# Time mixing: small triangles inverted as two halves at once, and the block between them by two products

## The chip, the cores and the metric

The kernel runs on one core of a Trainium2 chip. What counts is the device time of one execution in microseconds, as the median of several runs. The engines of a core are named as in the profile: PE is TensorE (PEld its weight loads), DVE is VectorE, ACT is ScalarE, POOL is GpSimd, SP is SyncE, which issues the transfers.

## The reference

Two layers of a streaming encoder, for a prompt of 1024 frames with 16 meta tokens ahead of it and for 64 frames of a running stream. Each layer projects the normalised input, sends the columns through three groups of heads side by side (a gated convolution, latent attention, time mixing), and projects the results back:

```python
z = h @ w_in
xin, bg, cg, ga, cq, ckv, kr, gb, zc, gc = jnp.split(z, IN_OFFSETS, axis=-1)
y_a = bg * conv * jax.nn.silu(ga)
y_b = o.reshape(b, t, MLA_W) * jax.nn.silu(gb)
y_c = yn.reshape(b, t, RWKV_W).astype(x.dtype) * jax.nn.silu(gc)
y = jnp.concatenate([y_a, y_b, y_c], axis=-1) @ w_out
return x + y
```

The change is in time mixing, a recurrence over the tokens with 4 heads of 64 by 64 state:

```python
def step(s, inp):
    r_t, w_t, k_t, v_t, kk_t, a_t = inp
    sa = jnp.einsum('bhvk,bhk->bhv', s, -kk_t)
    s = (s * w_t[:, :, None, :] + sa[..., None] * (kk_t * a_t)[:, :, None, :]
         + v_t[..., None] * k_t[:, :, None, :])
    return s, jnp.einsum('bhvk,bhk->bhv', s, r_t)
```

## The kernel before, in words

All tokens of both streams lie side by side, 1104 columns in three groups of up to 384 (`GROUPS`, line 36), features on the partitions. A layer begins with the projection (`project`, line 469): one block of 128 output columns for one token group is 24 matmuls into the tile `prj`, over 8 slices of the input with float32 split into a high and a low part (`whi`, `wlo`, `hhi`, `hlo`). The weights of a block come as `wraw`, and ScalarE and VectorE make `whi` and `wlo` of it. In `inproj_rest` (line 519) the blocks follow one another: the rest of the time mixing columns, gates, the latent columns `cq` and `ckv`, the rotary key `kr` (with `krt` and the weight `wkr`), the convolution (`xin`, `u`, `cv`), gates.

Time mixing runs beside this stream of projections. It is done in chunks of 64 tokens, in closed form within a chunk, and the chunks are chained by the state. `rwkv` (line 886) has three streams for it: `rwkv_prep` (line 922) prepares six parts a layer (three token groups of six chunks, for two pairs of heads), `rwkv_scan` walks the state through them (`xp`, `sp`, `state`, at the end `yp`), `rwkv_finish` does the group norm (`wq<-yp`, `gs`, then the turn `ym`). There are so 12 preparations in the kernel; they are counted here from the first of layer 0 to the twelfth, the seventh to twelfth being those of layer 1.

A preparation has to invert, for each of 12 chunk and head pairs, a unit upper triangular matrix of 64 by 64. It is done in levels. The four diagonal blocks of 16 by 16 come first: VectorE adds them out of the masked product into `dg` (line 1040), a trip through DRAM (`scr`) turns them round into `tri`, in which each of 48 partitions holds one 16 by 16 triangle, VectorE inverts them by rows (lines 1066 to 1070, 28 instructions for the 14 steps n), POOL sets the diagonal to one (line 1071), a copy makes the transpose, and another trip through DRAM brings both back as `dq` (named `dg` in the rows, whose tile it takes) and `dt`. VectorE spreads them with a mask to the block diagonal matrices `Q` (`wq<-dg`) and `Tm` (`wa<-dt`). Then TensorE joins blocks of 16 to 32 and 64 by products (`inv`), of which the first, `prod(A, Tm)` (line 1099, `inv<-wa` in the rows), needs `Tm`:

```python
        o = prod(A, Tm, self.psp("inv"))
```

What sets the order of the work: the kernel is written out by a Python program that keeps a model of each engine's time (`Meter`, lines 91 to 200). Each stream yields what its next step needs; `pump` (line 260) is called after each matmul of the projections and lets a stream of time mixing go on once the model says that what it needs is there. So the model decides how many `prj` matmuls stand between `tm<-cst,wb` (the last turn before the inversion, line 1063) and `inv<-wa`. On VectorE, ScalarE, POOL and SP the instructions are put in order once more when the program is built, by that framework's own estimate, so that the 28 do not stand in one piece.

The tile `lora` (line 929, one buffer) holds the two low-rank inputs of decay and learning rate. SP loads it at the start of a preparation, ScalarE passes half of it through a sigmoid in three steps, VectorE scales it, and two products read it; after them the preparation of before doesn't need it any more. `tri` and `lora` have one buffer each; attention, which comes later, uses both in turn for its weights.

Of the kernel before, what the change touches and what calls it, by code (L numbers as in the profile page):

```python
# [15 lines left out]
ALU = mybir.AluOpType  # L16
AX = mybir.AxisListType
# [14 lines left out]
GN = 384  # L32
# [4 lines left out]
BLK = 16  # L37
# [157 lines left out]
class Net:  # L195
# [726 lines left out]
    def rwkv_prep(self, l, i, g, hp):  # L922


        nc, I, O = self.nc, self.I, self.O
        tag = self.rwkv_tag(i)
        S = lambda s: self.S(tag, s)
        gc = slice(GN * g, GN * (g + 1))
        lora = self.small("lora", [128, 512])[:, :GN]
        nc.sync.dma_start(lora, self.zd[6, :, gc])  # L930
        wl = lora[0:64]
        self.sigmoid(wl, wl, 2.0)
# [2 lines left out]
        r, k, v = (wr[:, GN * x:GN * (x + 1)] for x in range(3))  # L935
# [14 lines left out]
        def turned(src, ts=range(3)):  # L950

            ps = rp("tm")
            for x, t in enumerate(ts):
                self.tr(ps[:, 128 * x:128 * (x + 1)], src(t), self.c(C_ID, 128))
            return ps[:, :GN].rearrange("p (t f) -> p t f", f=128)
# [3 lines left out]
        for t in range(3):  # L959
# [3 lines left out]
                                in0=ps[:, :GN].rearrange("p (t f) -> p t f", f=128),  # L963
                                in1=self.w0b[:, hc].unsqueeze(1).to_broadcast([128, 3, 128]), op=ALU.add)
# [16 lines left out]
        for t in range(3):  # L981
            tri = self.c(C_TRI0 if g == 0 and t == 0 else C_TRI, 128)
# [54 lines left out]
        for j in range(2):  # L1037
# [4 lines left out]
                                op=ALU.add, axis=AX.X)  # L1042
        scr = nc.dram_tensor(f"tri{l}_{g}_{hp}", (3, 6, 8, BLK, BLK), F32).ap()
        nc.sync.dma_start(scr[0].rearrange("t b r k -> (b r) t k"), dg)
        tri = self.small("tri", [128, 512])[:48].rearrange("p (i r k) -> p i r k", i=2, k=BLK)
        nc.sync.dma_start(tri[:, 0], scr[0].rearrange("t b r k -> (t b) r k"))
        yield kt, "rw"
        for ts in ((0, 1, 2), (3, 4, 5)):
            o = turned(lambda t: wx[:, 128 * t:128 * (t + 1)], ts)
# [10 lines left out]
        o = turned(lambda t: v[:, 128 * t:128 * (t + 1)])  # L1060
# [2 lines left out]
        nc.scalar.activation(at, turned(lambda t: wb[:, GN * t:GN * t + 128]), AF.Copy)  # L1063

        up, tm = tri[:, 0], tri[:, 1]
        for n in range(1, BLK - 1):
            o = [48, n, BLK - 1 - n]
            nc.vector.tensor_tensor(out=tm[:, :n, n + 1:], in0=up[:, :n, n:n + 1].to_broadcast(o), in1=up[:, n:n + 1, n + 1:].to_broadcast(o),
                            op=ALU.mult)
            nc.vector.tensor_tensor(out=up[:, :n, n + 1:], in0=up[:, :n, n + 1:], in1=tm[:, :n, n + 1:], op=ALU.add)  # L1070
        nc.gpsimd.memset(tri[:, 0].rearrange("p r k -> p (r k)")[:, 0:BLK * BLK:BLK + 1], 1.0)
        nc.vector.tensor_copy(tm, up.rearrange("p r k -> p k r"))
        nc.sync.dma_start(scr[1:3].rearrange("x t b r k -> (t b) x r k"), tri)
        dq, dt = dg, self.small("dt", [128, 6, BLK])
# [10 lines left out]
        def prod(lhs, rhs, ps, cc=slice(0, 64)):  # L1085
            o = ps[:, :GN].rearrange("p (t n) -> p t n", n=64)
            for t in range(6):
                for c in range(2):
                    self.mm(o[cr(c), t, cc], lhs[cr(c), t, :], rhs[cr(c), t, cc], start=True, stop=True)
            return o  # L1090
# [8 lines left out]
        o = prod(A, Tm, self.psp("inv"))  # L1099
# [13 lines left out]
        o = [x[:, :GN].rearrange("p (j t n) -> p j t n", j=2, n=64) for x in ps]  # L1113
# [13 lines left out]
        o = lambda c, j, x: ps[c][cr(j), 192 * x:192 * (x + 1)].rearrange("p (t n) -> p t n", n=64)  # L1127
        for j in range(2):
            for t, c in quad:
                b = cr(1 - c)  # L1130
# [404 lines left out]
```

## Time and profile before

| | us |
|---|---|
| median of 3 runs (1551.71 to 1553.72) | 1553.61 |
| the profiled execution, its own time | 1553.56 |
| its span in the profile | 1551.8 |
| PE busy (95% of the span, 12060 instructions) | 1476.9 |
| DVE busy (69%, 2623 instructions) | 1065.6 |
| ACT busy (50%) | 769.8 |
| POOL busy (17%) | 256.5 |

The profile is of one execution. The span runs from the first to the last instruction that it shows. Busy time is the time in which an engine had an instruction under way; PE's instructions overlap, so that a matmul of 384 columns lasts 0.34 us in a row and the next begins 0.175 us after it. The time in brackets behind a row is how long the engine was idle just before, and what ended that. Names are those of the program's tiles without numbers (`wq<-dg,cst` writes `wq` and reads `dg` and `cst`); nearly all instructions carry line 81, that of a helper, so tiles and shapes tell them apart. [...]

### The profile page before, as it was taken

To read this page: it belongs to the slowest core of one execution; us is meant where nothing else is said; L and a number is where in the kernel's file an instruction comes from. 1 tells how busy PE (TensorE), PEld (TensorE's weight loads), DVE (VectorE), ACT (ScalarE), POOL (GpSimd) and SP (SyncE) were. 2 spreads that over 40 slices of the span, in tenths; PEclk is the share of its full clock that TensorE was granted. 3 is DMA by queue.
4 is the path that set the end of the run, shared out by engine and by line. 5 is a ranking of instruction groups with operands and counts; after the bars stand their busy time and mean duration, and the time that the engine had idled before them with its cause. 6 is when DMAs were issued, how large, how long until landed. Compare 5 with 4: busy or idle time off the path is not lost.

```text
span 1551.8 us, 30755 instructions
## 1 busy us (share of the span) xinstructions
PE 1476.9 (95%) x12060; PEld 1311.2 (84%) x12060; DVE 1065.6 (69%) x2623; ACT 769.8 (50%) x1842; POOL 256.5 (17%) x281
## 2 busy tenths in 40 slices
PE   7999998998999999999999998899999999999996
PEld 7988887987887878879999887798988878778795
DVE  7576596675868766675845575776867787676566
ACT  7135454444577565563522354444356775565442
POOL 0221221311221101100011222312212301011002
PEclk9999999999999999999999999999999999999998
DMA  6332112222324101211323311212222331102123
GB/s 218 123 113 68 52 54 60 83 52 57 92 94 152 38 26 33 68 57 62 147 93 103 110 45 49 70 48 81 69 65 65 115 120 46 31 19 84 47 65 117
DMA packets 95328, 119.82 MB, mean 77 GB/s; under 512 B 41872, under 2 KB 74768, under 8 KB 95184
## 3 DMA queue, kind: packets, MB, share of 16 engines
q1 hardware_dynamic: 95184, 117.87, 24.6%
q8 instruction: 95, 1.56, 0.4%
q14 instruction: 49, 0.40, 0.1%
HBM read 81.24 MB, written 36.60 MB: 76 GB/s over the span
## 4 chain that ended last, share of the span: by engine, by line
PE 65%; DVE 17%; ACT 7%; issue 5%; DMA 3%; POOL 2%; SPq 0%; DVEq 0%; POOLq 0%; ACTq 0%
PE prj L81 31%; PE sc L81 7%; PE po L81 7%; PE tr L81 5%; PE upq L81 3%; DVE tri L81 3%; PE inv L81 2%; DVE wq L81 2%; PE val L81 1%; DVE wlo L81 1%; ACT wq L81 1%; PE upk L81 1%; DVE st L81 1%; DVE cv L81 1%; PE w L81 1%
## 5 line engine op out<-in xcount | busy, mean ns | idle before, releaser
L81 PE MATMUL prj<-hhi,whi 128*128 128x384 f32 (+1 forms) x1152 | 391.7, 340 | 7.5 <-ACT hhi L81 6.6
L81 PE MATMUL prj<-hlo,whi 128*128 128x384 f32 (+1 forms) x1152 | 390.7, 339 | 0.6 <-DVE hlo L81 0.6
L81 PE MATMUL prj<-hhi,wlo 128*128 128x384 f32 (+1 forms) x1152 | 390.4, 339 | 0.2 <-DVE wlo L81 0.2
L81 PEld LDWEIGHTS prj<-hhi,whi 128*128 128x128 f32 x1152 | 218.9, 190 | 11.0 <-ACT hhi L81 6.6
L81 PEld LDWEIGHTS prj<-hlo,whi 128*128 128x128 f32 x1152 | 218.7, 190 | 4.9 <-DVE hlo L81 1.0
L81 PEld LDWEIGHTS prj<-hhi,wlo 128*128 128x128 f32 x1152 | 218.7, 190 | 3.3 <-issue 0.5
L81 PE MATMUL prj<-yhi,wo 128*128 128x384 f32 (+2 forms) x776 | 207.0, 337 | 0.9 <-DVE xn L81 0.9
L81 PE MATMUL sc<-ka,qa 128*128 128x264 f32 (+8 forms) x720 | 152.4, 334 | 2.3 <-ACT p L81 2.0
L81 ACT ACTIVATE p<-sc,st 128x144 f32<-128x144 f32 (+8 forms) x240 | 128.1, 542 | 50.4 <-DVE st L81 49.3
L81 PEld LDWEIGHTS prj<-yhi,wo 128*128 128x128 f32 x776 | 138.4, 188 | 4.8 <-DVE xn L81 2.4
L81 DVE TENSOR_REDUCE st<-sc 128x1 f32<-128x144 f32 (+8 forms) x240 | 118.0, 502 | 24.3 <-PE sc L81 22.4
L81 PE MATMUL prj<-ylo,wo 128*128 128x384 f32 (+2 forms) x388 | 130.6, 337 | 0.0
L81 ACT ACTIVATE pt<-tr 128x512 f32<-128x512 f32 (+3 forms) x172 | 90.0, 544 | 77.6 <-PE tr L81 76.3
L81 PEld LDWEIGHTS sc<-ka,qa 128*128 128x128 f32 (+1 forms) x720 | 112.2, 187 | 19.0 <-ACT p L81 6.1
L81 PE MATMUL tr<-cst,p 128*128 128x128 f32 (+2 forms) x752 | 115.7, 277 | 3.3 <-ACT pt L81 1.7
L81 PE MATMUL po<-pt,v 128*64 128x256 f32 (+3 forms) x864 | 110.7, 357 | 0.0
L81 PEld LDWEIGHTS tr<-cst,p 128*128 128x128 f32 (+2 forms) x752 | 83.5, 140 | 25.6 <-issue 7.6
L81 POOL TENSOR_TENSOR qa<-qt,qa 128x512 fp32r<-128x512 f32 (+1 forms) x40 | 47.3, 1184 | 349.3 <-ACT qa L81 349.3
L81 ACT ACTIVATE whi<-wraw 128x1024 fp32r<-128x1024 f32 x48 | 50.7, 1056 | 82.6 <-PE prj L81 64.9
L81 DVE TENSOR_TENSOR tri<-tri 48x14 f32<-48x14 f32 (+6 forms) x336 | 82.2, 245 | 9.1 <-DMA tri<-tri 0.3
L81 PEld LDWEIGHTS po<-pt,v 128*64 128x64 f32 (+1 forms) x864 | 56.6, 136 | 33.5 <-issue 11.6
L81 DVE TENSOR_SCALAR p<-p,st 80x336 f32<-80x336 f32 (+5 forms) x144 | 81.5, 568 | 1.9
(227 smaller groups left out, 2639.9 us busy)
## 6 DMA issues: line engine op xcount, KB each, us to landing
wraw<-w_in SPq DMA_DIRECT2D x48, 512.0 KB, 3.6
wraw<-w_out SPq DMA_DIRECT2D x32, 256.0 KB, 2.6
zd<-z SPq DMA_DIRECT2D x14, 576.0 KB, 3.4
wr<-zd SPq DMA_DIRECT2D x36, 192.0 KB, 3.0
gd<-gate SPq DMA_DIRECT2D x12, 552.0 KB, 3.1
yraw<-yd SPq DMA_DIRECT2D x8, 552.0 KB, 4.0
xn<-x SPq DMA_DIRECT2D x8, 552.0 KB, 3.9
xd<-xn SPq DMA_DIRECT2D x8, 552.0 KB, 3.0
```

What stands on the lines that cost most here:

```text
L81: r = f(*args, **kw)
```

## The change

The triangle of 16 by 16 is taken as two of 8 by 8 on the diagonal and a block of 8 by 8 between them. The row by row steps run over both halves in the same instruction (6 steps n, 12 instructions). The block between is then multiplied by the one inverse and by the other: each product is one multiplication of 512 elements a partition and one reduction over the last 8, 4 instructions. The scratch for all of this is the tile `lora`, of which the first 48 partitions are used; before, the scratch was the half `tm` of `tri` itself. The memset of the diagonal stands ahead of the loop, since the products need it.

```diff
-        lora = self.small("lora", [128, 512])[:, :GN]
+        room = self.small("lora", [128, 512])
+        lora = room[:, :GN]
...
         up, tm = tri[:, 0], tri[:, 1]
-        for n in range(1, BLK - 1):
-            o = [48, n, BLK - 1 - n]
-            nc.vector.tensor_tensor(out=tm[:, :n, n + 1:], in0=up[:, :n, n:n + 1].to_broadcast(o), in1=up[:, n:n + 1, n + 1:].to_broadcast(o),
-                            op=ALU.mult)
-            nc.vector.tensor_tensor(out=up[:, :n, n + 1:], in0=up[:, :n, n + 1:], in1=tm[:, :n, n + 1:], op=ALU.add)
-        nc.gpsimd.memset(tri[:, 0].rearrange("p r k -> p (r k)")[:, 0:BLK * BLK:BLK + 1], 1.0)
+        flat, room = tri.rearrange("p i r k -> p (i r k)"), room[:48]
+        nc.gpsimd.memset(flat[:, 0:BLK * BLK:BLK + 1], 1.0)
+        h = BLK // 2
+        two = flat[:, 0:2 * (h * BLK + h)].rearrange("p (b x) -> p b x", b=2)[:, :, 0:h * BLK].rearrange("p b (r k) -> p b r k", k=BLK)[:, :, :, 0:h]
+        for n in range(1, h - 1):
+            o = [48, 2, n, h - 1 - n]
+            part = room[:, 0:2 * n * (h - 1 - n)].rearrange("p (b r k) -> p b r k", b=2, r=n)
+            nc.vector.tensor_tensor(out=part, in0=two[:, :, :n, n:n + 1].to_broadcast(o), in1=two[:, :, n:n + 1, n + 1:].to_broadcast(o), op=ALU.mult)
+            nc.vector.tensor_tensor(out=two[:, :, :n, n + 1:], in0=two[:, :, :n, n + 1:], in1=part, op=ALU.add)
+        cube = room[:, 0:h * h * h].rearrange("p (i k j) -> p i k j", i=h, k=h)
+        between, mid = up[:, 0:h, h:], tm[:, 0:h, 0:h]
+        for x, y, o in ((between, up[:, h:, h:], mid), (up[:, 0:h, 0:h], mid, between)):
+            nc.vector.tensor_tensor(out=cube, in0=x.unsqueeze(2).to_broadcast([48, h, h, h]),
+                                    in1=y.rearrange("p j k -> p k j").unsqueeze(1).to_broadcast([48, h, h, h]), op=ALU.mult)
+            nc.vector.tensor_reduce(out=o, in_=cube, op=ALU.add, axis=AX.X)
         nc.vector.tensor_copy(tm, up.rearrange("p r k -> p k r"))
```

The model that places the matmuls sees other instructions, and so other rows follow on all engines. Three places.

VectorE, third preparation of layer 0, around the end of the inversion (`tri`, `lora`; the copy makes the transpose, `kr` and `krt` are the rotary key). Before:

```order
L81 TENSOR_TENSOR kr_2323<-kr_2323 32x384
L81 TENSOR_TENSOR tri_2219<-tri_2219 48x11x4
L81 TENSOR_TENSOR wlo_2408<-wraw_2321,whi_2407 128x1024
L81 TENSOR_TENSOR tri_2219<-tri_2219 48x12x3
L81 TENSOR_TENSOR wr_1419<-xp_2434,wq_1430 64x128
L81 TENSOR_TENSOR tri_2219<-tri_2219 48x12x3
L81 COPY u_2405<-par_79 128x2
L81 MEMSET u_2405 128x2
L81 TENSOR_TENSOR tri_2219<-tri_2219 48x13x2 x2
L81 TENSOR_TENSOR tri_2219<-tri_2219 48x14 x2
L81 COPY tri_2219<-tri_2219 48x256
L81 TENSOR_TENSOR wq_2069<-dg_2216,cst 128x6x64
```

And with the change:

```order
L81 SCALAR_TENSOR_TENSOR kr_2308<-krt_2309,rot 32x336
L81 TENSOR_REDUCE tri_2181<-lora_2011 48x8x8
L81 SCALAR_TENSOR_TENSOR krt_2309<-krt_2309,rot 32x336
L81 TENSOR_TENSOR lora_2011<-tri_2181 48x512
L81 TENSOR_TENSOR kr_2308<-kr_2308,krt_2309 32x336
L81 TENSOR_REDUCE tri_2181<-lora_2011 48x8x8
L81 TENSOR_TENSOR krt_2309<-prj_2333,krt_2309 64x384
L81 COPY tri_2181<-tri_2181 48x256
L81 TENSOR_TENSOR krt_2309<-prj_2356,krt_2309 64x384
L81 SCALAR_TENSOR_TENSOR kr_2308<-krt_2309,rot 32x384
L81 TENSOR_TENSOR kr_2308<-kr_2308 32x256
L81 SCALAR_TENSOR_TENSOR krt_2309<-krt_2309,rot 32x384
```

Before, the copy stands behind all of the rotary work and `wq<-dg` comes next; now the copy stands ahead of most of it, and 13 instructions come between the copy and `wq<-dg`. Between the first instruction of the inversion and the copy stood 22 others, and now 13.

TensorE, the same preparation, the end of the stretch before `inv<-wa` (`prj` matmuls of a projection, `sp` of the scan). Before:

```order
L81 MATMUL prj_2513<-hhi_140,wlo_2408 128x336
L81 MATMUL prj_2513<-hhi_141,whi_2407 128x336
L81 MATMUL prj_2513<-hlo_149,whi_2407 128x336
L81 MATMUL prj_2513<-hhi_141,wlo_2408 128x336
L81 MATMUL prj_2513<-hhi_142,whi_2407 128x336
L81 MATMUL prj_2513<-hlo_150,whi_2407 128x336
L81 MATMUL inv_2529<-wa_2068 64x64 x12
```

And with the change:

```order
L81 MATMUL prj_2515<-hlo_154,whi_2392 128x336
L81 MATMUL prj_2515<-hhi_146,wlo_2393 128x336
L81 MATMUL prj_2542<-hhi_139,whi_2392 128x384
L81 MATMUL prj_2542<-hlo_147,whi_2392 128x384
L81 MATMUL inv_2545<-wa_2027 64x64 x12
```

Before, the first inversion product stood in the eighth part of a group of 24 `prj` matmuls; now that group is done and the next begun. From `tm<-cst,wb` to there stood 124 `prj` matmuls, and now 146.

SP, first preparation of layer 0 (`wraw` a weight load, `zd` the shifted columns, `tri_0_0` the scratch in DRAM). Before:

```order
L81 DMA zd<-z_677 128x1152
L81 DMA lora_1413<-zd 128x384
L81 DMA wraw_923<-w_in 128x1024
L81 DMA zd<-z_784 128x1152
L81 DMA wr_1419<-zd 128x384
L81 DMA tri_0_0<-dg_969 128x6x16
L81 DMA wr_1419<-zd 128x384 x2
L81 DMA tri_972<-tri_0_0 48x256
```

And with the change:

```order
L81 DMA zd<-z_784 128x1152
L81 DMA wr_1400<-zd 128x384
L81 DMA tri_0_0<-dg_969 128x6x16
L81 DMA wr_1400<-zd 128x384 x2
L81 DMA tri_972<-tri_0_0 48x256
L81 DMA lora_1394<-zd 128x384
L81 DMA o_shift<-sh_156 128x14
L81 DMA wraw_1089<-w_in 128x1024
L81 DMA tri_0_0<-tri_972 48x2x256
```

The load of `lora` for the second preparation stood ahead of the first one's transfers; now it stands behind the load of `tri` and ahead of a weight load.

## Rows read from the trace of the kernel before

**Rows 1.** The page, busy us (share of the span) and instructions.

```profile
PE 1476.9 (95%) x12060; PEld 1311.2 (84%) x12060; DVE 1065.6 (69%) x2623; ACT 769.8 (50%) x1842; POOL 256.5 (17%) x281
```

**Rows 2.** The page, chain that ended last by line, share of the span.

```profile
PE prj L81 31%; PE sc L81 7%; PE po L81 7%; PE tr L81 5%; PE upq L81 3%; DVE tri L81 3%; PE inv L81 2%; DVE wq L81 2%; PE val L81 1%; DVE wlo L81 1%; ACT wq L81 1%; PE upk L81 1%; DVE st L81 1%; DVE cv L81 1%; PE w L81 1%
```

**Rows 3.** Waits of TensorE: us in total, times, longest us.

```profile
PE inv L81 <- DVE wa L81: 12.1, 3, 5.3
PE xp L81 <- DVE state L81: 7.6, 11, 1.6
...
PE ym L81 <- DVE wq L81: 5.9, 3, 2.4
```

**Rows 4.** Timeline of TensorE: start us, us, instruction, [idle before, what ended it].

```profile
238.59 1.43 PE L81 MATMUL inv<-wa 64*64 64x64 f32 x21 [5.33 <-DVE wa L81]
...
359.38 0.85 PE L81 MATMUL inv<-wa 64*64 64x64 f32 x21 [1.65 <-DVE wa L81]
...
1003.83 1.43 PE L81 MATMUL inv<-wa 64*64 64x64 f32 x21 [5.16 <-DVE wa L81]
```

**Rows 5.** Stretches: length, busy us of PE, PEld, DVE, ACT, POOL, PEclk, DMA, GB/s.

```profile
234.00:238.50 4.50, 0.00 (x0) 0.00 (x0) 1.08 (x3) 1.01 (x2) 1.99 (x2) 0.63 0.29 44
238.50:242.00 3.50, 3.41 (x51) 3.08 (x52) 2.25 (x5) 0.78 (x2) 0.00 (x0) 0.50 0.33 80
...
1003.50:1006.50 3.00, 2.67 (x48) 2.42 (x48) 1.98 (x4) 0.78 (x2) 0.00 (x0) 0.50 0.24 29
```

**Rows 6.** Timeline of VectorE, third preparation of layer 0.

```profile
212.90 0.16 DVE L81 TENSOR_TENSOR tri<-tri 48x14 f32<-48x14 f32 x1
...
232.75 0.37 DVE L81 COPY tri<-tri 48x256 f32<-48x256 f32 x1
237.22 0.56 DVE L81 TENSOR_TENSOR wq<-dg,cst 128x384 f32<-128x384 f32 x1 [4.10 <-DMA dg<-tri]
237.98 0.56 DVE L81 TENSOR_TENSOR wa<-dt,cst 128x384 f32<-128x384 f32 x1 [0.20 <-DMA dt<-tri]
238.45 1.22 DVE L81 TENSOR_TENSOR wlo<-wraw,whi 128x1024 fp32r<-128x1024 f32 x1
```

**Rows 7.** Groups of instructions: count, busy us, mean ns, idle before; then by form.

```profile
L81 DVE TENSOR_TENSOR tri<-tri 48x14 f32<-48x14 f32 (+6 forms) x336 | 82.2, 245 | 9.1 <-DMA tri<-tri 0.3
...
L81 DVE TENSOR_TENSOR tri<-tri 48x14 f32<-48x14 f32 x48 | 9.8, 204 | 1.5 <-DMA tri<-tri 0.3
L81 DVE TENSOR_TENSOR tri<-tri 48x26 f32<-48x26 f32 x48 | 8.5, 177 | 1.4
```

**Rows 8.** Groups by form, reductions of VectorE.

```profile
L81 DVE TENSOR_REDUCE st<-sc 128x1 f32<-128x512 f32 x32 | 22.0, 688 | 7.2 <-PE sc L81 6.8
...
L81 DVE TENSOR_REDUCE dg<-wq 128x96 f32<-128x384 f32 x12 | 9.7, 807 | 0.0
```

**Rows 9.** Timeline of TensorE, first and last of 20 matmuls of 384 columns.

```profile
227.69 0.34 PE L81 MATMUL prj<-hlo,whi 128*128 128x384 f32 x1
...
231.02 0.34 PE L81 MATMUL prj<-hhi,wlo 128*128 128x384 f32 x1
```

**Rows 10.** Timeline of VectorE and TensorE, first preparation of layer 0.

```profile
119.87 0.56 DVE L81 TENSOR_TENSOR wa<-dt,cst 128x384 f32<-128x384 f32 x1 [0.36 <-DMA dt<-tri]
...
122.23 0.85 PE L81 MATMUL inv<-wa 64*64 64x64 f32 x21
```

**Rows 11.** Stretches of time mixing beside the projections, layer 0 and layer 1.

```profile
95.00:465.00 370.00, 347.46 (x3432) 317.94 (x3433) 257.77 (x639) 180.60 (x409) 82.73 (x92) 0.99 0.25 71
856.00:1226.00 370.00, 348.36 (x3427) 319.51 (x3427) 257.87 (x636) 181.26 (x408) 83.20 (x92) 0.98 0.24 69
```

**Rows 12.** Waits of ScalarE for the tile `lora`; its loads, issue to landing.

```profile
ACT lora L81 <- DMA lora<-zd: 21.8, 5, 12.7
...
DMA to landing us min/median/max: 2.3/2.4/5.6
```

## The prediction

> **What bounds the kernel now.** I read the page's busy shares first. TensorE works 1476.9 us of a span of 1551.8 us and VectorE 1065.6 [rows 1]; so at most 74.9 us, TensorE's idle time, can be won by waiting less, and VectorE time that nobody waits for is worth nothing. The chain that ended last gives 3% to the `tri` instructions [rows 2]; that would be 46 us, but the chain names whatever stood before a late instruction, and `tri` sits on it also where TensorE had other work. The list of TensorE's own waits is the sharper view: the product `inv<-wa`, the first that needs the inverted triangles, waited for VectorE 3 times, 12.1 us in all; the scan's `xp` 7.6 us in 11 pieces; the group norm's `ym` 5.9 us [rows 3]. In time order the three are 5.33 us at 238.59 (third preparation of layer 0), 1.65 at 359.38 (fifth) and 5.16 at 1003.83 (third of layer 1) [rows 4]. In the other nine preparations the triangles come back before TensorE asks for them.
>
> [...]
>
> Why did the third preparation wait? VectorE starts the inversion at 212.90 and ends the copy behind it at 233.12. Between the inversion's 28 instructions stand 22 others, most of them rotary work on `kr` and `krt`. Then VectorE idles 4.10 us until the result has gone through DRAM and back, and `wa` is written at 238.54 [rows 6]. TensorE had 124 `prj` matmuls to cover this and stood still 5.33 us before 238.59 [rows 4].
>
> **The change part by part.**
>
> *The instructions.* All 336 old ones (12 preparations by 28) take 82.2 us, so 6.9 us an inversion [rows 7]. The new: 12 small ones, two multiplications over 512 elements and two reductions of 512. The small ones have 12 to 24 elements; nearest are the forms of 14 and 26 elements, 204 and 177 ns [rows 7]: 12 x 0.19 = 2.3 us. For the multiplications, float32 with both operands in SBUF took 0.56 us for 384 elements and 1.22 for 1024 [rows 6]; a line through both gives 0.69 for 512. A reduction of 512 took 0.69 from PSUM, and one of 384 to 96 results with strided reads 0.81, which is 1.08 for 512 [rows 8]. So the cheap end is 2.3 + 4 x 0.69 = 5.1 us, 1.8 less than now. The dear end prices both multiplications and reductions by the strided reduction: 2.3 + 4 x 1.08 = 6.6, only 0.3 less. I take 1.0 less, inside these; over 12 preparations that is 12 us of VectorE, nearly all under TensorE's work.
>
> [...]
>
> *The copy, the four small transfers and the diagonal's memset* stay; the memset moves ahead of the loop and waits for the same load: nothing.
>
> *The order.* The kernel places matmuls by estimated times, so other work now lies between. In the third preparation of either layer the stretch from `tm<-cst,wb` to `inv<-wa` holds 146 `prj` matmuls instead of 124, and 24 `yp` ones besides. From 227.69 to 231.02 are 19 steps, 0.175 us each [rows 9]: 22 x 0.175 = 3.9 us more cover. On VectorE 13 instead of 22 others stand inside the inversion; the rotary rest stands behind the copy, where VectorE idled 4.10 us [rows 6]. Filling that saves up to 4.1 us of the path, less a `wq<-yp` addition and its reduction that now come in (384 elements each, 2 x 0.56 by [rows 6]), so 3.0; with the 1.0 from above 4.0. Cover and path together are 7.9 us, against waits of 5.33 and 5.16: both go, -10.5 us. Even at the dear end (0.3 instead of 1.0) 7.2 are left.
>
> The fifth preparation loses 7 `prj` (107 for 114, 1.2 us) and gains 1.0, plus 1.2 because a `wlo` (1.22 [rows 6]) no longer stands between copy and use: 1.65 + 1.2 - 1.0 - 1.2 = 0.65 us remain, -1.0 us.
>
> Who is late next? The preparations that lose matmuls. The tightest is the first: `wa` is ready at 120.43, TensorE asks at 122.23, a margin of 1.80 [rows 10]; it loses 7 `prj`, 1.2 us, so 0.6 remains before the inversion's own gain. The fourth loses most, 25 (4.4 us), the eleventh 13, the second 12, the eighth 8, the seventh 6, each from a wider margin. I count no new wait on `wa`.
>
> *The clock.* The 3.4 and 2.7 us that TensorE worked at half clock after the two long waits [rows 5] would take half: -3.0 us.
>
> *The group norm.* Ahead of `ym` the second and eighth preparations now have 70 `prj` for 29; of the 5.9 us [rows 3] the longest wait, 2.4, belongs to the fifth, the other 3.5 to these two and go. The order ahead of `ym` in the fifth (few `prj` behind `yp`) now stands in the eleventh also: +2.4. Together -1.1 us.
>
> *Other waits in the new order.* The two layers do the same work in partly different orders. Over equal stretches of 370 us TensorE worked 347.46 and 348.36 us [rows 11], so a change of order by itself moved about 1 us. I allow +1.5 us a layer, +3.
>
> *A new order of loads.* The scratch for the products is the tile `lora`, which the next preparation loads again. Its load now waits on SP until the last product is read, with a weight load and the transfers behind it. The next use of that tile is a whole preparation away, so I cost it at nothing; the cover is that distance, and what it costs without cover is the second rival.
>
> The sum: -10.5 - 1.0 - 3.0 - 1.1 + 3 = -12.6 us. The profiled execution took 1553.56 us, which is its span of 1551.8 and 1.8 around it, and the median of the three runs shown is 1553.61; so **1541 us**.
>
> **The rivals.**
>
> *Only the inversion's own length counts.* The matmuls that now cover the third preparations were taken from others, 25 from the fourth alone; if waits open there, the order gives back what it took. Then only the path is shorter, by 0.3 to 1.8 us in the three preparations that waited: 1 to 5 us, so 1548 to 1552.6. For it speaks that TensorE's work is the same; against it the margins above. [...]
>
> *The shared scratch blocks SP and ScalarE (slower).* The three `lora` activations stand in ScalarE's queue behind that load, and evictions of `prj` stand behind them. The load lands 2.4 us after issue [rows 12]. If ScalarE stands that long in the ten preparations that have a successor, and TensorE's PSUM banks fill, that is up to 24 us: 1541 + 24 = 1565. It makes the kernel slower by over 0.2% from 1.6 us each on. For it: on SP the load now stands ahead of a weight load. Against it: before, ScalarE stood 21.8 us in 5 pieces for exactly this load, 12.7 at the longest [rows 12], and TensorE's list has no wait that this explains.
>
> **How the numbers follow.** 0.2% is 3.1 us, about what a measurement here can tell from no change: 1550.5 to 1556.7. My forecast has a chance of 0.72, and its own range is 1535 (no new waits, `ym` gone in the fifth too) to 1547 (twice the allowance, inversion at the dear end). The first rival has 0.18, half of it below 1550.5; the second 0.10, of which 0.02 falls within 0.2%. Faster: 0.70 + 0.09 = 0.79; same: 0.02 + 0.09 + 0.02 = 0.13; slower: 0.08. The range that holds 8 in 10 runs from 1533 to 1551, which leaves out the second rival and the upper half of the first.
>
> **What would show it.** In the profile after: 192 instructions with `tri` and `lora` in place of 336, 5.1 to 6.6 us an inversion; no wait of `inv<-wa` above 1 us in the third preparations, and no stretch of half clock there; TensorE idle about 65 us for 74.9 (the clock's 3.0 are not idle time); `ym` waits in the fifth and eleventh. I am wrong if `inv<-wa` still waits several us, if rows of TensorE waiting for `whi`, `z` or `cq` evictions appear behind a `lora` load, or if idle time stays at 75 us under other names.

## The result, and the profile after

The changed kernel took 1544.24 us (median of 6 runs, 1541.18 to 1547.6), the kernel before 1553.66 beside it (6 runs, 1551.71 to 1555.56): a ratio of 0.994, 95% interval 0.9925 to 0.9954. It is faster by 9.4 us; 12.6 were predicted, and the range held it. The profiled execution is the longest of the six, 1547.6 us with a span of 1545.8, so the traces lie 6.0 us apart: the rows below are an account of these 6.0 us, not of the 9.4.

The page, busy us of each engine:

```profile
PE 1478.2 (96%) x12060; PEld 1316.8 (85%) x12060; DVE 1062.5 (69%) x2480; ACT 770.5 (50%) x1841; POOL 262.5 (17%) x281
```

TensorE's idle time is 1545.8 - 1478.2 = 67.6 us, where it was 74.9 [rows 1]; its busy time rose by 1.3. The waits of TensorE (us in total, times, longest):

```profile
PE tm L81 <- ACT wa L81: 7.7, 4, 2.1
PE inv L81 <- DVE wx L81: 6.6, 4, 3.0
...
PE xp L81 <- DVE state L81: 4.5, 5, 2.6
...
PE ym L81 <- DVE wq L81: 4.0, 6, 0.9
PE tr L81 <- ACT pt L81: 3.7, 4, 1.0
PE inv L81 <- ACT gs L81: 3.6, 2, 1.8
PE inv L81 <- DVE wa L81: 3.6, 3, 2.2
PE sc L81 <- ACT p L81: 3.3, 4, 1.2
...
PE inv L81 <- ACT sq L81: 1.6, 1, 1.6
...
PE yp L81 <- DVE state L81: 0.4, 2, 0.2
```

The rows of the same view before that answer to these and do not stand in [rows 3]:

```profile
PE tm L81 <- ACT wa L81: 6.7, 4, 3.4
...
PE inv L81 <- DVE wx L81: 4.2, 4, 1.6
PE yp L81 <- DVE state L81: 3.7, 6, 1.1
PE sc L81 <- ACT p L81: 2.0, 6, 0.4
PE inv L81 <- ACT ka L81: 1.9, 2, 1.0
PE tr L81 <- ACT pt L81: 1.7, 2, 0.9
```

So `inv<-wa` fell from 12.1 [rows 3] to 3.6 us, `xp` from 7.6 to 4.5, `ym` from 5.9 to 4.0, and `yp` from 3.7 to 0.4. Longer are the waits of `inv` for `wx` and those of attention's `tr` and `sc`; new are those of `inv` for `gs` and `sq`. The timeline of TensorE shows where:

```profile
175.73 0.82 PE L81 MATMUL inv<-wa 64*64 64x64 f32 x21 [1.58 <-ACT sq L81]
...
237.72 0.85 PE L81 MATMUL inv<-wa 64*64 64x64 f32 x21
...
244.20 1.54 PE L81 MATMUL inv<-wq,wa 64*64 64x64 f32 x24 [3.04 <-DVE wx L81]
...
300.05 0.85 PE L81 MATMUL inv<-wa 64*64 64x64 f32 x21 [0.70 <-DVE wa L81]
304.51 1.00 PE L81 MATMUL inv<-wq,wa 64*64 64x64 f32 x24 [1.82 <-ACT gs L81]
...
934.45 0.82 PE L81 MATMUL inv<-wa 64*64 64x64 f32 x21 [2.17 <-DVE wa L81]
```

The row at 237.72 is the third preparation: the wait of 5.33 us [rows 4] is gone, and so is that of the ninth. But 6 us later, in the same preparation, the second product waits 3.04 us, and the second (175.73), the eighth (934.45), the fourth (300.05) and, by the same 0.70, the tenth wait where they had not.

VectorE, third preparation of layer 0:

```profile
223.35 0.36 DVE L81 COPY tri<-tri 48x256 f32<-48x256 f32 x1
...
231.71 2.02 DVE L81 TENSOR_TENSOR wlo<-wraw,whi 128x1024 fp32r<-128x1024 f32 x1
...
235.51 0.55 DVE L81 TENSOR_TENSOR wq<-dg,cst 128x384 f32<-128x384 f32 x1
...
236.44 0.55 DVE L81 TENSOR_TENSOR wa<-dt,cst 128x384 f32<-128x384 f32 x1
...
240.35 1.23 DVE L81 TENSOR_TENSOR wlo<-wraw,whi 128x1024 fp32r<-128x1024 f32 x1 [0.39 <-ACT whi L81]
...
242.13 1.46 DVE L81 SCALAR_TENSOR_TENSOR cv<-u,par,cv 128x64 f32<-128x64 f32 x2
243.51 1.01 DVE L81 TENSOR_TENSOR wx<-x,cst 128x384 f32<-128x384 f32 x2
```

The copy ends at 223.71, 9.4 us earlier in the span than before [rows 6], of which 1.5 are an earlier start. The rotary work now stands behind it and holds `wq<-dg` until 235.51, and `wa` ends at 236.98. Five of the 13 instructions in between are stretched, such as the `wlo` of 2.02 us (the later one takes 1.23); each of the five ran beside a GpSimd instruction, the last two beside this pair:

```profile
231.64 2.96 POOL L81 TENSOR_TENSOR xin<-xin,rs 128x384 f32<-128x384 f32 x2 [0.37 <-ACT xin L81]
```

The backlog goes on behind `wa`: `wlo`, a convolution step and only then `wx`, for which the second product waits.

The groups of the new instructions by form (count, busy us, mean ns), and ScalarE's wait for the shared scratch:

```profile
L81 DVE TENSOR_TENSOR lora<-tri 48x512 f32<-48x512 f32 x24 | 27.5, 1144 | 1.3
L81 DVE TENSOR_REDUCE tri<-lora 48x64 f32<-48x512 f32 x24 | 16.1, 672 | 0.2
...
ACT lora L81 <- DMA lora<-zd: 35.6, 9, 12.6
```

With the 144 small ones (30.9 us) the 192 instructions take 74.5 us, 6.2 an inversion where it was 6.9. The clock, stretches of the new trace (length, busy us of PE, PEld, DVE, ACT, POOL, PEclk, DMA, GB/s; PEclk is the granted share of TensorE's clock, 1.00 or 0.50 in every record of the traces before and after):

```profile
243.75:247.17 3.42, 2.97 (x49) 2.88 (x50) 0.88 (x3) 0.00 (x0) 1.71 (x2) 0.50 0.41 134
305.19:308.61 3.42, 3.42 (x40) 2.87 (x37) 1.15 (x3) 0.67 (x1) 0.20 (x1) 0.50 0.13 44
1001.51:1008.34 6.83, 5.37 (x73) 4.84 (x75) 2.83 (x5) 0.30 (x1) 2.72 (x3) 0.50 0.30 101
```

All three are at 0.50, and each stands behind or around one of the new waits. In the two stretches of time mixing together the trace before has 24 us at 0.50 and this one 27; the mean clock of the profiled execution is 0.989 before, 0.986 here and 0.984 in the profile of the changed kernel taken again. The waits of 1.58 us (175.73) and 2.17 us (934.45) have no such stretch behind them, PEclk is 1.00 there, so these runs don't show which waits bring one.

Read by stage, us and TensorE's idle us in brackets, with two of the experiments. Time mixing begins with the first `ldp` product of a layer, attention goes from its first `sc` product to its last one, and the rest ends with TensorE's last instruction:

| | mixing 0 | attention 0 | to layer 1 | mixing 1 | attention 1 | rest |
|---|---|---|---|---|---|---|
| before | 378.2 (22.4) | 233.3 (3.6) | 148.3 (0.0) | 380.3 (22.7) | 233.7 (3.6) | 87.8 (4.2) |
| changed | 374.6 (17.9) | 234.1 (5.1) | 149.4 (0.0) | 373.5 (17.1) | 234.8 (4.8) | 89.2 (3.8) |
| old 28, new order | 371.8 (17.2) | 235.0 (4.9) | 149.4 (0.0) | 373.5 (17.3) | 235.0 (5.0) | 89.2 (3.7) |
| new 16, old order | 377.4 (21.3) | 233.8 (3.7) | 148.3 (0.0) | 372.8 (19.1) | 233.4 (3.6) | 88.2 (3.7) |

The changed kernel wins 3.6 and 6.8 us in mixing and gives 1.9 and 2.5 back behind it: the order of attention moved as well, 20 `val` products and two of `sp` out of mixing into it, and 14 `prj` from attention into the stage after.

### The profile page after: what moved, and what is told of

Its sections match the earlier page's. It is cut to its first block, busy times and chain, and to the rows that moved or that the text cites. A ratio compares the mean times of both kernels' runs of the same rounds, so it can differ in the third digit from the quotient of the medians.

```text
span 1545.8 us, 30613 instructions
## 1 busy us (share of the span) xinstructions
PE 1478.2 (96%) x12060; PEld 1316.8 (85%) x12060; DVE 1062.5 (69%) x2480; ACT 770.5 (50%) x1841; POOL 262.5 (17%) x281
## 4 chain that ended last, share of the span: by engine, by line
PE 67%; DVE 17%; ACT 7%; issue 5%; POOL 2%; DMA 1%; SPq 0%; DVEq 0%; POOLq 0%; ACTq 0%
PE prj L81 33%; PE sc L81 7%; PE po L81 7%; PE tr L81 5%; PE upq L81 3%; PE inv L81 2%; DVE wq L81 2%; DVE lora L81 2%; PE val L81 1%; DVE tri L81 1%; PE tm L81 1%; ACT wq L81 1%; ACT sil L81 1%; PE w L81 1%; DVE kr L81 1%
## 5 line engine op out<-in xcount | busy, mean ns | idle before, releaser
L81 PE MATMUL sc<-ka,qa 128*128 128x512 f32 (+9 forms) x720 | 156.3, 337 | 4.4 <-ACT p L81 3.3
L81 DVE TENSOR_REDUCE st<-sc 128x1 f32<-128x144 f32 (+8 forms) x240 | 117.7, 502 | 24.0 <-PE sc L81 22.3
L81 PE MATMUL po<-pt,v 128*64 128x256 f32 (+3 forms) x864 | 106.8, 356 | 0.0
L81 DVE TENSOR_TENSOR wlo<-wraw,whi 128x1024 fp32r<-128x1024 f32 x48 | 69.1, 1439 | 16.2 <-ACT whi L81 13.8
```

The lines of the kernel that those rows point to most:

```text
L81: r = f(*args, **kw)
```

## The experiments

Theory: the gain is the waits of the third preparations, through the order of the matmuls and the shorter inversion together. Rivals: the inversion's length alone; the shared scratch as a cost. The first two runs part the change: the instructions of one kernel, TensorE's order of the other, by telling the model of the instructions that are not issued. VectorE's own queue is put in order when the program is built, so in both it is that of neither kernel.

**Old 28 instructions in the new order.**

```diff
+        old(Both(nc.nc.vector, nc.nc.gpsimd), room)
+        new(Both(Noted('vector'), Noted('gpsimd')), room)
```

> The 28 old instructions, but the model that places the matmuls is told of the 16 new ones, so that TensorE's order is that of the changed kernel (264 of 9646 rows differ). If the moved matmuls bring the gain: 1541 to 1547 us, the third preparations without a wait of inv<-wa over 1 us. If the shorter inversion brings it: back near 1553, with waits of some us in the third and the second preparations.

Measured: 1545.53 us, ratio 0.9954 (0.9939 to 0.9969). TensorE's waits in it:

```profile
PE inv L81 <- DVE wa L81: 11.6, 5, 4.0
...
PE inv L81 <- DVE wx L81: 4.2, 3, 2.0
...
PE ym L81 <- DVE wq L81: 2.6, 4, 1.3
PE xp L81 <- DVE state L81: 1.9, 5, 0.8
```

The order without the new instructions makes the kernel faster by some 7 us although the third preparations still wait 3.92 and 3.96 us for `wa`: with 28 instructions 14.8 us of other work stand before the copy. Its gain is in the scan and the group norm (`xp` 7.6 to 1.9, `ym` 5.9 to 2.6, `yp` 3.7 to 0.4). And TensorE's idle time is 66.4 us (span 1544.2, busy 1477.8), no more than the 67.6 of the changed kernel: in this order the 16 instructions take 8.0 us from `inv<-wa`, and `xp`, `wx`, `ym` and `sq` take it back.

**New 16 instructions in the old order.**

```diff
+        new(Both(nc.nc.vector, nc.nc.gpsimd), room)
+        old(Both(Noted('vector'), Noted('gpsimd')), room)
```

> The 16 new instructions, but the model is told of the 28 old ones, so that TensorE's order is that of before (38 of 9646 rows differ). If the moved matmuls bring the gain: 1550 to 1554 us, and inv<-wa in the third preparations still waits 3 to 5 us. If the shorter inversion brings it: 1542 to 1547.

Measured: 1545.2 us, ratio 0.9962 (0.9948 to 0.9977). The page, the waits of TensorE, and one stretch:

```profile
PE 1473.9 (95%) x12060; PEld 1307.6 (85%) x12060; DVE 1065.7 (69%) x2479; ACT 773.2 (50%) x1842; POOL 255.3 (17%) x281
...
PE xp L81 <- DVE state L81: 9.1, 11, 1.8
PE ym L81 <- DVE wq L81: 7.5, 4, 2.8
...
PE yp L81 <- DVE state L81: 5.8, 7, 1.6
...
PE inv L81 <- DVE wa L81: 4.2, 3, 1.7
...
236.72:242.00 5.28, 3.73 (x92) 3.31 (x94) 3.10 (x6) 2.49 (x5) 3.64 (x3) 1.00 0.34 104
```

Without any new cover the instructions take `inv<-wa` from 12.1 to 4.2, 1.74 in each third preparation, and the clock after that wait stays at 1.00 where it was 0.50 [rows 5]. The path from `tm<-cst,wb` to `wa` became 3.0 us shorter in the third preparations (27.2 to 24.2 in layer 0), more than the 1.9 that the inversion's own instructions lost there. VectorE's queue is another too: 12 other instructions stand inside the inversion and 11 behind its copy, where 22 and none did. What the shorter instructions do without that was not run. Here the clock's part of the forecast came true: TensorE's busy time fell by 3.0 us, with 10 us at half clock in mixing for 24. Idle time fell by 4.9 only, since `xp`, `ym` and `yp` rose. So either half brings 6 to 7 us, and both together 9.4, not 14: they draw on the same idle time. The intervals of the two halves and of the changed kernel (0.9925 to 0.9954) overlap, so these runs don't show that both together beat either one.

**A scratch of its own for the products**, in a buffer of attention; the model is still told of `lora`.

```diff
+        new(Both(nc.nc.vector, nc.nc.gpsimd), self.sp.tile([128, 512], F32, tag="pt", name=self.nm("cube"), bufs=JOBS))
+        new(Both(Noted('vector'), Noted('gpsimd')), room)
```

> The changed kernel with the products' scratch in a tile that attention uses later, not in lora; the model's account is kept. The next load of lora is then issued ahead of the inversion, as before. If the shared tile costs time: ScalarE's waits for lora fall from 35.6 us to about 22 and the kernel gets 1 to 5 us faster than the changed one (1539 to 1543). If it costs nothing: 1543 to 1546.

Measured: 1547.69 us, ratio 0.9967 (0.9953 to 0.9981). ScalarE's wait for the load fell as it should:

```profile
ACT lora L81 <- DMA lora<-zd: 21.2, 3, 12.9
```

From 35.6 to 21.2 us, and the kernel gained nothing by it: its time lies above both expected ranges. In its profile, one of its longer executions, `inv` waits 10.5 us for `wx` and 6.1 for `wa` (6.6 and 3.6 in the changed kernel); why is not shown. The shared tile makes ScalarE wait 14 us longer, under cover, as the prediction had it; the second rival falls.

**Contiguous products.** The multiplication reads its second operand in steps of one and each element of the first eight times over, and writes in steps of one; the reduction reads in steps of 8.

```diff
-        cube = room[:, 0:h * h * h].rearrange("p (i k j) -> p i k j", i=h, k=h)
+        cube = room[:, 0:h * h * h].rearrange("p (i j k) -> p i j k", i=h, j=h)
...
+            nc.vector.tensor_reduce(out=o, in_=cube.rearrange("p i j k -> p i k j"), op=ALU.add, axis=AX.X)
```

> The changed kernel with the scratch laid out so that the multiplication reads both operands and writes its result in steps of one element, and the reduction reads in steps of eight; same order of instructions on all engines. If the step of 16 elements in its second operand is what makes the multiplication 1.06 us instead of the 0.69 I took: it falls to about 0.65, the reduction stays 0.67 or rises to 1.1. If the repeated reading of the first operand is the cause: 1.06 stays. The time: 1541 to 1545, since nearly all of this is under TensorE's work.

Measured: 1548.1 us, ratio 0.9977 (0.9967 to 0.9987). Groups by form:

```profile
L81 DVE TENSOR_REDUCE tri<-lora 48x64 f32<-48x512 f32 x24 | 27.7, 1156 | 0.2
L81 DVE TENSOR_TENSOR lora<-tri 48x512 f32<-48x512 f32 x24 | 18.2, 757 | 1.3
```

The steps moved from one instruction to the other, and so did the time: 27.5 + 16.1 before, 18.2 + 27.7 here. The interval lies above that of the changed kernel, and the time above the expected 1541 to 1545; why the whole is slower at nearly the same sum of the two stays open.

**Strided write**, beside the changed kernel on the same chip. The multiplication reads as in the contiguous products and writes in steps of 8; the reduction reads in steps of one.

```diff
-            nc.vector.tensor_tensor(out=cube, in0=x.unsqueeze(2).to_broadcast([48, h, h, h]),
-                                    in1=y.rearrange("p j k -> p k j").unsqueeze(1).to_broadcast([48, h, h, h]), op=ALU.mult)
+            nc.vector.tensor_tensor(out=cube.rearrange("p i k j -> p i j k"), in0=x.unsqueeze(3).to_broadcast([48, h, h, h]),
+                                    in1=y.unsqueeze(1).to_broadcast([48, h, h, h]), op=ALU.mult)
```

> The changed kernel as it is, beside the next three on the same chip, since the two runs of it so far and the four variants stood on different chips. Theory (the gain comes from the third preparations, where cover absorbs an unchanged path, and from the scan): 1543 to 1546 us, with inv<-wa waits of 3 to 4 us in all and inv<-wx of about 6 to 7 us. Rival (part of the first result was the chip): 1547 or more, ratio 0.996 or above.

> The four long instructions of an inversion read in steps of 1 everywhere: the multiplication takes both operands contiguous and writes its result in steps of 8, the reduction reads contiguous. The order on every engine is that of the changed kernel. Theory (reads in steps cost twice, writes in steps cost nothing): the multiplication falls from about 1.06 to 0.67 us, the reduction stays at 0.67, an inversion from 6.2 to 5.4 us. Rival (writes in steps cost as much as reads): multiplication stays at 1.04 or more. For the time: theory that VectorE's length matters only where TensorE waits: third preparations have no inv<-wa wait anyway, so the 0.8 us is worth 0 to 3 us in all, within 1540 to 1546 us; rival that the inversion's length is what counts everywhere: 12 x 0.8 = 9 us, 1535 us.

Measured: the changed kernel again 1545.79 us, ratio 0.9944 (0.9927 to 0.9962); the strided write 1545.05, 0.9943 (0.9929 to 0.9957). The changed kernel's first result stands. The theory that a write in steps costs nothing fell:

```profile
L81 DVE TENSOR_TENSOR lora<-tri 48x512 f32<-48x512 f32 x24 | 30.2, 1258 | 1.3
```

The write in steps of 8 took no less than the read in steps of 16. The means are 1258 ns here, 1144 as changed and 757 with no steps; the two multiplications of the third preparation of layer 0 took 1.16 us each here, 1.04 and 1.07 as changed and 0.68 each with no steps. So the inversion was not made shorter, and what a shorter one would bring in this order was not measured.

**The spreads first**, alone and with the strided write.

```diff
+        with self.tc.high_priority():
             for y, d, o in ((1, dq, Q), (2, dt, Tm)):
...
+        with self.tc.high_priority():
             nc.vector.copy_predicated(Q, mk(0), oq)
             nc.vector.copy_predicated(Tm, mk(1), ot)
             for j in range(2):
                 masked(j)
```

> The changed kernel, with the two spreads (wq<-dg and wa<-dt), the two predicated copies and the masked wx put ahead of other ready work on VectorE. In the third preparations wa then stands ahead of one rotary step, a group norm addition and a reduction. Theory (cover already absorbs the path there): wa is ready about 2 us earlier, nothing waits less for it, and the group norm's ym waits move by less than 1 us each: 1543 to 1547 us, inside the control's interval. Rival (the backlog on VectorE behind the spreads is what makes the next product wait 3.0 us for wx): that wait falls in both third preparations by 1 us or more each, 1539 to 1542 us.

> Both edits of the two runs ahead of it together, as the version that might beat both kernels. Theory: the gains are not additive and small, 1540 to 1546 us, TensorE idle 63 to 68 us. Rival: shorter inversion and earlier spreads each free VectorE's queue in the third preparations, so that both the 3.0 us waits for wx go: 1536 to 1540 us.

Measured: 1547.67 us, 0.9959 (0.9943 to 0.9976), and 1546.98, 0.9949 (0.9933 to 0.9964). TensorE's waits in the first:

```profile
PE inv L81 <- DVE wx L81: 6.6, 4, 3.0
...
PE yp L81 <- DVE state L81: 5.7, 4, 2.7
...
PE inv L81 <- ACT gs L81: 0.4, 1, 0.4
```

In the third preparation `wa` stands earlier in VectorE's queue, and the wait for `wx` is the same 3.04 us; `wlo` and the convolution step still stand before it, so this edit did not try what moving them would do. The 3.6 us of `gs` went, and `yp` rose from 0.4 to 5.7. With both edits `wx` waits 6.6 us as well, and TensorE is idle 69.0 us, where 63 to 68 were expected.

**The old order with the strided write**, alone and with the two spreads first. The edits are those of the new 16 in the old order and of the strided write; the second has besides:

```diff
+        with self.tc.high_priority():
             for y, d, o in ((1, dq, Q), (2, dt, Tm)):
```

> The new 16 instructions in the order of the kernel before (as in the run of that name), and the multiplications read contiguous and write in steps of 8. The order on TensorE is that of the old order with the new instructions, row by row. Here the third preparations still wait for wa, 1.74 us each, so that a shorter inversion has something to give. Theory (VectorE's length counts where its path is the later of the two): inv<-wa falls from 4.2 us in 3 to about 2 us in all (0.8 less in each of the three), 1542 to 1545 us, ratio 0.993 to 0.996, the same as or up to 2 us better than the changed kernel. Rival (the 0.8 us moves into the waits behind, as in the new order): 1545 to 1548 us.

> The same kernel, with the two spreads wq<-dg and wa<-dt put ahead of other ready work on VectorE. In the fifth and in the second preparation wa then stands ahead of a group norm step; the third preparations do not change. Theory: the fifth's wait for wa (0.69 us) goes and its longest ym wait (2.8 us) changes by less than 1 us: within 1.5 us of the run beside it. Rival (a group norm step that comes later costs its whole length of 0.56 us and more at ym): 1 to 3 us slower than the run beside it.

Measured: 1544.9 us, 0.9951 (0.9937 to 0.9966), and 1547.13, 0.9958 (0.9943 to 0.9973). In the first, page and waits:

```profile
PE 1471.4 (95%) x12060; PEld 1305.7 (85%) x12060; DVE 1066.2 (69%) x2479; ACT 772.9 (50%) x1842; POOL 256.1 (17%) x281
...
PE inv L81 <- DVE wa L81: 4.1, 3, 1.7
```

The multiplication did not become shorter here either, so `inv<-wa` stays, and TensorE's idle time is 71.7 us (span 1543.1); its busy time is lower still. In the second, the fifth preparation's wait for `wa` went (4.1 us in three to 3.5 in two), and `ym` rose from 7.3 to 8.7, the longest from 2.8 to 3.6. That is the rival's sign; the two times differ by 2.2 us, and their intervals overlap. The intervals of the changed kernel and of the variants but the contiguous product overlap: none beats it by what these runs can tell.

## Why the prediction was right, and where it was not

**The bound.** That only TensorE's 74.9 idle us could be won held: about 65 were forecast to be left, 67.6 and, in the profile of the changed kernel taken again, 65.9 (1546.4 - 1480.5) were.

**The third preparations, -10.5.** Both waits went. The term has its size, but not by its two parts, and that is luck. Cover from `tm<-cst,wb` to `inv<-wa`, without the wait at its end, was 21.9 us before and is 28.9, so 7.0 more and not 3.9: only the `prj` were counted, not the 24 `yp` and what stands with them. The path to `wa` was to be 4.0 us shorter; it went from 27.2 to 28.1. The step "Filling that saves up to 4.1 us of the path" failed. Of the 13 instructions behind the copy only the group norm's addition was priced. Together they took 11.3 us and ran until 235.51, while `dt<-tri`, the later of the two loads, was issued at 226.21 and landed 2.2 us later. Of the 11.3 some 3.7 are the stretch of five of them beside GpSimd; without it they would still have ended past the load, by an estimate from these rows. (Inside the inversion the trace has 11 others, not 13.) Against the same order with the 28 (32.1 us) the path is 4.0 shorter.

**"I count no new wait on `wa`"** failed. The second and eighth preparations, with margins of 3.94 and 3.37 us before, now wait 1.58 and 2.17, and the fourth and tenth 0.70 each. (In the second the profile names `sq`; `wa` was there only 0.15 us ahead of the product, as in the eighth.) Again it was `prj` alone that was counted: 12 fewer were 2.1 us, while the second's whole cover fell from 22.3 to 17.7. Of the 4.6, TensorE's work gave 2.8, and 1.8 was a wait for the group norm, which had been cover too and is gone. The tenth shows this best: its margin before, 1.66 us, was the tightest of all, and it gained 3 `prj` and 6 `yp`, but 2.7 us of waits inside its stretch went, and its path became 1.1 longer. The fourth lost 5.0 us of cover, and its path became 3.6 longer, which was not looked at. The fifth was better than forecast: its wait is gone.

**The clock, -3.0,** did not come: busy time rose by 1.3 us (by 3.6 in the profile taken again). The half clock behind the two long waits went, but stretches of it stand at the shorter new waits of 1.8 to 3.0 us. Where the long waits became short without new ones, in the old order, busy time fell by the forecast 3.0. It also shows from run to run: the six runs of the changed kernel go from 1541.18 at a mean clock of 0.991 to 1547.6 at 0.986.

**The group norm, -1.1,** was -1.9; no wait there is above 0.9 us, where 2.4 were foreseen in the eleventh. **Other waits, +3:** `wx`, `gs`, `tm` and attention's `sc` and `tr` rose by 10.3 together, `xp`, `yp` and `inv<-ka` fell by 8.3, so +2.0; the 1.58 of `sq` is counted above, with the waits for `wa`. As a sum the allowance was near, but by luck: it was a small difference of large moves, and the scan's part of it is, by the run of the old instructions, the main gain of the new order by itself.

**The inversion** was to take 5.9 us and takes 6.2, inside the ends of 5.1 and 6.6. The reductions cost 0.67 (0.69 taken), so they were not the slow part, and the twelve small ones 2.6 together for 2.3. The mis-sized piece is the multiplication: 0.69 was taken from contiguous operands, and with one operand in steps of 16 it costs 1.07 (the median), near the dear end's 1.08. In the contiguous run it took 0.68 us in the third preparation of layer 0, close to the 0.69 taken.

**The rivals.** That only the length counts (1548 and more) is refuted: the order without the shorter instructions gives 7 us. Its price looks too low as well: with the new instructions in TensorE's old order the path became 3.0 us shorter in each third preparation, where it had 0.3 to 1.8, and the kernel gained 5.9 us (3.6 to 8.1), where it had 1 to 5. Its reason was half right, though: covers taken from the second and fourth did open waits. The shared scratch as a cost is refuted by the run with its own.

## What to carry to other kernels

In a kernel whose matmuls are placed by a model of the engines, an edit to one engine's instructions is two edits, and the moved order can be worth as much as the shorter work; run each without the other before crediting either. When counting cover, count all work of the waiting engine between two points, not the commonest kind, and its other waits there, which can go; do it for every stretch that loses some. Work pushed behind a critical step in an engine's queue is the delay of the next one (here 11.3 us of VectorE ahead of `wq<-dg`): add up its length, and name what waits for that too.

## What was not expected of the hardware

A float32 multiplication on VectorE over 512 elements took 0.68 us with no steps in its operands and 1.16 with the result written in steps of 8 (both in the third preparation of layer 0), and 1.07 with one read in steps of 16 (the median of 24); a reduction took 0.67 contiguous and 1.16 in steps of 8 (the means). Moving the steps between reads and writes did not lose them.

VectorE instructions took longer beside GpSimd ones. In the first preparation the copy behind the inversion took 2.28 us instead of 0.37, beside a GpSimd instruction that took 3.62 itself, where the same one took 2.11 at 51.17 (timelines of the changed kernel):

```profile
110.39 3.62 POOL L81 TENSOR_TENSOR zd<-z 128x1151 f32<-128x1151 f32 x1 [7.63 <-issue]
...
111.97 2.28 DVE L81 COPY tri<-tri 48x256 f32<-48x256 f32 x1
```

The copy ends at 114.25, 0.24 us after the GpSimd instruction at 114.01. What ties the two is not shown. The kernel before met the same GpSimd instruction earlier, inside its inversion, where one of the 28, 0.19 us long in the row before, took 2.16:

```profile
108.03 2.16 DVE L81 TENSOR_TENSOR tri<-tri 48x50 f32<-48x50 f32 x1
...
108.03 2.11 POOL L81 TENSOR_TENSOR zd<-z 128x1151 f32<-128x1151 f32 x1 [5.00 <-DVE tri L81]
```

So both kernels lost about 2 us here. The inversion ends at 110.85 with the change and at 114.48 before, and the copy behind it at 114.25 and 114.90: of 3.6 us, 0.65 are left behind the copy, since a `wlo` of 1.20 us and the stretched copy come in between.
